# Softplus for the forget gates, a spread start of the first head, four staging buffers for weights, and new places for casts and a scaling

## The chip, the cores and the metric

The kernel runs on one core of a Trainium2 chip. The core has five engines with queues of their own: TensorE (PE, matmuls; PEld is its loading of weights), VectorE (DVE), ScalarE (ACT), GpSimd (POOL) and SyncE (SP), which here issues all DMA transfers. Each engine works off its queue in the order in which the program was laid out, and waits on semaphores for the others. The metric is the device time of one execution in microseconds; given is the median of three executions.

## The reference

Two pre-norm residual layers on a sequence of 1024 rows of width 1024, in float32, and a final RMS norm. The first layer is a gated linear recurrence (RG-LRU, width 1536), the second attention with forget gates (FoX, 16 heads of 64).

```python
def lru_mixer(h, w_in, conv_w, conv_b, wa, ba, wx, bx, a_param, w_out):
    u = h @ w_in
    xb, gate = u[..., :LRU_WIDTH], u[..., LRU_WIDTH:]
    xc = causal_depthwise_conv(xb, conv_w, conv_b)
    r = jax.nn.sigmoid(block_diag_linear(xc, wa, ba))
    i = jax.nn.sigmoid(block_diag_linear(xc, wx, bx))
    log_a = -LRU_C * r * jax.nn.softplus(-a_param)
    a = jnp.exp(log_a)
    mult = jnp.sqrt(-jnp.expm1(2.0 * log_a))
    # hs: h_t = a_t * h_(t-1) + mult_t * i_t * xc_t
    y = hs * jax.nn.silu(gate)
    return y @ w_out

def fox_mixer(h, w_in, b_f, w_out):
    u = h @ w_in                                  # q, k, v, gate, f_logit
    cum = jnp.cumsum(jax.nn.log_sigmoid(f_logit + b_f), axis=1)
    # for each head and block of 128 queries:
    logits = q @ k.T / 8 + (cum_q[:, None] - cum_k[None, :])
    p = jax.nn.softmax(jnp.where(kpos <= qpos, logits, -1e30))
    y = (p @ v) * jax.nn.silu(gate)
    return y @ w_out
```

## The kernel before

**Arithmetic.** Each float32 operand of a large product is split into a high part (a cast, `to_hi`, line 88 on ACT, 94 or 96 on DVE) and a low part, the remainder (`to_lo`, line 99, on DVE or POOL). A product then is three matmuls: high by high, high by low, low by high. All go through `matmul` (line 57) and `transpose` (line 61), so that these lines stand for every matmul of the kernel, and the tile names tell them apart: `ups` and `gps` are inner projections, `gate` the block-diagonal gates of the recurrence, `ops` output projections, `S` the scores, `pt` transposed probabilities, `O` the products of probabilities and values.

**Weights.** `split_weights` (line 101) loads a weight tile into a staging tile `wf`, casts it to `wh` and takes the remainder `wl`. The staging tiles rotate through three buffers under one tag; the same tag is used for the gate weights `wgf` of the recurrence (line 287), the output weights of the first layer (line 352) and the late output weights of the second (line 951). A load that finds no free buffer waits on SP, with all later transfers of SP's queue behind it.

**Attention.** `forget(half)` (line 622) transposes the gate logits of 512 positions into PSUM, forms the logarithm of the sigmoid as min(z, 0) − ln(1 + exp(−|z|)) with three activations and two DVE steps, accumulates it with a scan into `cum`, splits it (`cp`) and writes it to DRAM (`cumd`), from where `load` and `load_q` fetch it as rows 64 and 65 of the operands `T` and `U` of the scores. For each head `maxima(hd, c)` (line 684) makes scores `S` for four blocks of 128 queries, masks them and takes the row maximum in one DVE instruction (line 707), and takes the exponential `p` on ACT (line 712). p(384) below means the block whose p has 384 columns. `weigh(hd, c)` transposes p through PE, splits it into `ph` and `pl`, and multiplies with the values. `scale(hd)` multiplies, on POOL, the gate `sg` by the reciprocal row sums `recb`; `gated` multiplies the head pair's output `yo` by it, on POOL too. Results of the first six head pairs are written to DRAM (`y1d`) and fetched again by `load_y`; those of the last two are split at once by `split_y` into `yhh` and `yhl`.

**Order.** A scheduler places the instructions of all engines by its own simulated timeline; so the place of an instruction in an engine's queue follows from costs and free buffers, not from the order of the code alone. The pool's buffers are part of that. `tc.issue_after(x)` keeps what is in its block behind x; `pe[0]` is the last matmul, `seen[0]` the last exponential of `maxima`. Around this the code weaves generators by hand: `run(order, ...)` takes one character per step, a digit for a step of that generator, a dot for a step of `fill`, which is projection work of later heads (`kq_units`, `g_units`) or, at heads 12 to 15, the output projection (`partial`), and then drains the digit generators. `beside(steps, first, more)` takes a step of `more` with each step from number `first` on. `split_loaded(c)` splits the fetched y tiles, two pairs a step. `values` loads and multiplies the values of four heads; it runs at the end of heads 3, 7 and 11.

## Time and profile before

| | us |
|---|---|
| median of three executions | 1123.55 |
| lowest, highest | 1122.89, 1124.05 |
| profiled execution | 1125.28 |
| its span in the profile | 1123.4 |
| outside the span | 1.88 |

The mean granted clock of TensorE in the profiled execution is 0.997. In the rows of the profile an engine's busy time is given with the number of instructions behind an x; a row of the timeline has its start and length in us, engine, line, operation, output and input with sizes, and in square brackets how long the engine stood idle just before and what ended that.

### The profile page before, as it was taken

To read this page: it belongs to the slowest core of one execution; us is meant where nothing else is said; L and a number is where in the kernel's file an instruction comes from. 1 tells how busy PE (TensorE), PEld (TensorE's weight loads), DVE (VectorE), ACT (ScalarE), POOL (GpSimd) and SP (SyncE) were. 2 spreads that over 40 slices of the span, in tenths; PEclk is the share of its full clock that TensorE was granted. 3 is DMA by queue.
4 is the path that set the end of the run, shared out by engine and by line. 5 is a ranking of instruction groups with operands and counts; after the bars stand their busy time and mean duration, and the time that the engine had idled before them with its cause. 6 is when DMAs were issued, how large, how long until landed. Compare 5 with 4: busy or idle time off the path is not lost. (4 is left out here: it accounts for less than half of the span.)

```text
span 1123.4 us, 15748 instructions
## 1 busy us (share of the span) xinstructions
PE 1106.5 (98%) x5681; PEld 933.0 (83%) x5681; DVE 764.6 (68%) x1271; ACT 589.3 (52%) x1077; POOL 166.5 (15%) x105
## 2 busy tenths in 40 slices
PE   8999999999999999999999999999999999999997
PEld 6787888888888887978888988889888898878886
DVE  7889756776568789666676466764566745676645
ACT  8387445355453666455555355553555534554435
POOL 1311212221121201320010100102001010010110
PEclk9999999999999999999999999999999999999999
DMA  6111111111111114443425214252142431655454
GB/s 218 52 43 51 43 62 38 52 52 44 60 38 52 57 57 144 127 123 100 105 76 133 71 57 119 73 127 81 40 127 79 124 87 38 182 175 162 146 155 187
DMA packets 63702, 105.43 MB, mean 94 GB/s; under 512 B 9508, under 2 KB 24484, under 8 KB 63624
## 3 DMA queue, kind: packets, MB, share of 16 engines
q1 hardware_dynamic: 63624, 104.42, 31.0%
q8 instruction: 45, 0.74, 0.3%
q14 instruction: 33, 0.27, 0.1%
HBM read 63.30 MB, written 15.93 MB: 71 GB/s over the span
## 5 line engine op out<-in xcount | busy, mean ns | idle before, releaser
L57 PE MATMUL gps<-hh,wh 128*128 128x512 f32 x576 | 227.9, 396 | 1.4 <-DVE qkl L585 1.4
L57 PE MATMUL gps<-hl,wh 128*128 128x512 f32 x576 | 225.6, 392 | 0.0
L57 PE MATMUL gps<-hh,wl 128*128 128x512 f32 x576 | 225.5, 391 | 0.0
L88 ACT CAST wh<-wf 128x512 fp32r<-128x512 f32 (+2 forms) x156 | 94.5, 607 | 157.8 <-PE gps L57 48.8
L712 ACT ACTIVATE p<-S,m 128x128 f32<-128x128 f32 (+7 forms) x128 | 95.0, 742 | 124.5 <-DVE m L707 123.6
L99 POOL TENSOR_TENSOR wl<-wf,wh 128x512 fp32r<-128x512 f32 (+1 forms) x60 | 98.1, 1641 | 388.5 <-ACT wh L88 337.4
L99 DVE TENSOR_TENSOR pl<-pt,ph 128x512 fp32r<-128x512 f32 (+1 forms) x198 | 98.7, 540 | 74.4 <-ACT ph L88 73.9
L57 PEld LDWEIGHTS gps<-hl,wh 128*128 128x128 f32 x576 | 108.1, 188 | 23.5
L57 PEld LDWEIGHTS gps<-hh,wh 128*128 128x128 f32 x576 | 108.4, 188 | 20.4 <-DVE qkl L585 1.6
L57 PEld LDWEIGHTS gps<-hh,wl 128*128 128x128 f32 x576 | 108.5, 188 | 19.3 <-POOL wl L99 0.6
L707 DVE CUSTOM_DVE_ANT_0 S<-S,mask 128x128 f32<-128x128 f32 (+7 forms) x128 | 97.2, 760 | 30.5 <-PE S L57 26.0
L739 POOL TENSOR_TENSOR sg<-sg,recb 64x1024 f32<-64x1024 f32 (+1 forms) x17 | 38.9, 2288 | 451.1 <-DMA recb<-recd 415.0
L88 ACT CAST ph<-pt 128x512 fp32r<-128x512 f32 (+1 forms) x198 | 83.5, 472 | 29.7 <-PE pt L61 24.4
L57 PE MATMUL S<-T,U 96*128 96x512 f32 (+7 forms) x384 | 91.9, 348 | 1.8 <-ACT p L712 1.7
L99 DVE TENSOR_TENSOR wl<-wf,wh 128x512 fp32r<-128x512 f32 x96 | 70.4, 735 | 32.0 <-ACT wh L88 31.1
L369 DVE TENSOR_TENSOR x<-x,ops 128x512 f32<-128x512 f32 x80 | 54.1, 682 | 45.6 <-PE ops L57 45.6
L57 PEld LDWEIGHTS S<-T,U 128*128 128x128 f32 (+1 forms) x384 | 68.1, 189 | 15.8 <-ACT p L712 4.2
L61 PE MATMUL pt<-ident,p 128*128 128x128 f32 x576 | 79.5, 273 | 0.4 <-ACT p L712 0.4
L57 PE MATMUL ups<-hh,wh 128*128 128x512 f32 x192 | 75.8, 396 | 2.4 <-ACT hh L90 2.0
L61 PEld LDWEIGHTS pt<-ident,p 128*128 128x128 f32 x576 | 67.1, 140 | 13.3 <-issue 2.2
L57 PE MATMUL ops<-yh,wh 128*128 128x512 f32 x192 | 75.4, 393 | 1.2 <-ACT yh L88 0.6
L57 PE MATMUL ups<-hl,wh 128*128 128x512 f32 x192 | 76.1, 396 | 0.3 <-DVE hl L242 0.2
(177 smaller groups left out, 2258.1 us busy)
## 6 DMA issues: line engine op xcount, KB each, us to landing
wf<-in_w SPq DMA_DIRECT2D x100, 256.0 KB
wf<-in_wo SPq DMA_DIRECT2D x64, 128.0 KB
U<-qkh SPq DMA_DIRECT2D x64, 128.0 KB
T<-qkh SPq DMA_DIRECT2D x28, 256.0 KB
x<-in_xt SPq DMA_DIRECT2D x16, 256.0 KB
x1d<-x SPq DMA_DIRECT2D x16, 256.0 KB
wf<-in_wv SPq DMA_DIRECT2D x16, 256.0 KB
U<-qkl SPq DMA_DIRECT2D x32, 128.0 KB
```

The source lines that it names most:

```text
L57: pe[0] = nc.tensor.matmul(*args, **kw)
L61: pe[0] = nc.tensor.transpose(*args)
L88: nc.scalar.copy(hi, src)
L99: return eng.tensor_tensor(lo, src, f32(hi), ALU.subtract)
L369: nc.vector.tensor_tensor(x, x, pt, ALU.add)
L707: nc.vector.tensor_tensor_reduce(S[:, :n], S[:, :n], mask[:, SEQ - n :], -1.0, -NEG, ALU.add, ALU.min, accum_out=m)
L712: seen[0] = nc.scalar.activation(p, S[:, :n], AF.Exp, bias=m, scale=-1.0, accum_out=sums[:, i : i + 1])
L739: nc.gpsimd.tensor_tensor(sg, sg, recs[hd // 2][rows, cs], ALU.mult)
```

## The change

There are six parts:

- The staging tiles `wf` and `wgf` rotate through four buffers in place of three, at the four places named.
- `forget` negates the bias once on DVE and takes ln(1 + exp(−z)) as one Softplus straight out of PSUM; the scan subtracts it.
- The first head's `maxima(0, 0)` is made before the first fill begins and its steps are spread over two fills; `ordered` is `run` without the draining at the end.
- `scale` works in parts of 512 columns.
- `split_loaded` yields after each pair; the steps at which it begins are 0 and 2 in place of 2 and 4.
- The two calls of `split_y` at heads 13 and 14 stand behind the last exponential.

```diff
--- before.py
+++ after.py
@@ -101,7 +101,7 @@
     def split_weights(src, shape, hi_eng, lo_eng, parts=wpool):
         n = shape[0] * shape[1]
         room = -(-n // 64) * 64
-        a = wpool.tile([P, room], F32, tag="wf", name="wf", bufs=3)[:, :n]
+        a = wpool.tile([P, room], F32, tag="wf", name="wf", bufs=4)[:, :n]
         b = parts.tile([P, room], F32R, tag="wh", name="wh")[:, :n]
         c = parts.tile([P, room], F32R, tag="wl", name="wl")[:, :n]
         wt, hi, lo = (t.rearrange("p (a b) -> p a b", a=shape[0]) for t in (a, b, c))
@@ -284,7 +284,7 @@
             xh, xl = long("xch", F32R), long("xcl", F32R)
             to_hi(xh, xc, nc.scalar)
             to_lo(xl, xc, xh, nc.vector)
-            wt = wpool.tile([P, 4, P], F32, tag="wf", name="wgf", bufs=3)[:, :2]
+            wt = wpool.tile([P, 4, P], F32, tag="wf", name="wgf", bufs=4)[:, :2]
             nc.sync.dma_start(wt, wg[n])
             wgh = tmp.tile([P, 2, P], F32R, tag="wgh", name="wgh")
             wgl = tmp.tile([P, 2, P], F32R, tag="wgl", name="wgl")
@@ -349,7 +349,7 @@
 
         def out_weights(g, d0):
 
-            wt = wpool.tile([P, 4, P], F32, tag="wf", name="wf", bufs=3)
+            wt = wpool.tile([P, 4, P], F32, tag="wf", name="wf", bufs=4)
             for j in range(2):
                 nc.sync.dma_start(wt[:, 2 * j : 2 * j + 2], wo0[d0 + j, :, 2 * g : 2 * g + 2])
             hi = wpool.tile([P, 4, P], F32R, tag="wh", name="wh")
@@ -615,6 +615,7 @@
         Vs = {}
         bft = const.tile([HEADS, 1], F32, name="bft")
         nc.sync.dma_start(bft, bf)
+        nc.vector.tensor_scalar(bft, bft, -1.0, None, ALU.mult)
         unit = at.tile([HEADS, HALF], F32, tag="recb", name="unit", bufs=1)
         nc.gpsimd.memset(unit, 1.0)
         cum = at.tile([HEADS, SEQ], F32, tag="sg", name="cum")
@@ -627,16 +628,12 @@
                     yield
                 with tc.issue_after(pe[0].ins):
                     transpose(pt[:HEADS, i * P : (i + 1) * P], fz[:, half * 4 + i], ident)
-            z_, e_ = (at.tile([HEADS, HALF], F32, tag=t, name=n, bufs=3) for t, n in (("ph", "z"), ("pl", "e")))
+            e_ = at.tile([HEADS, HALF], F32, tag="ph", name="e", bufs=3)
             parts = [at.tile([HEADS, HALF], F32R, tag=f"p{i + 2 * half}", name="cp", bufs=1) for i in (3, 4)]
             hi, lo = parts
-            nc.scalar.activation(z_, pt[:HEADS], AF.Identity, bias=bft)
-            nc.vector.scalar_tensor_tensor(e_, z_, -1.0, z_, ALU.mult, ALU.min)
-            nc.scalar.activation(e_, e_, AF.Exp)
-            nc.scalar.activation(e_, e_, AF.Ln, bias=1.0)
-            nc.vector.scalar_tensor_tensor(z_, z_, 0.0, e_, ALU.min, ALU.subtract)
+            nc.scalar.activation(e_, pt[:HEADS], AF.Softplus, bias=bft, scale=-1.0)
             nc.vector.tensor_tensor_scan(
-                cum[:, cs], unit, z_, cum[:, HALF - 1 : HALF] if half else 0.0, ALU.mult, ALU.add
+                cum[:, cs], unit, e_, cum[:, HALF - 1 : HALF] if half else 0.0, ALU.mult, ALU.subtract
             )
             to_hi(hi, cum[:, cs], nc.vector)
             to_lo(lo, cum[:, cs], hi, nc.vector)
@@ -735,8 +732,10 @@
 
         def scale(hd, cs=slice(0, SEQ)):
             rows = slice((hd % 2) * HD, (hd % 2 + 1) * HD)
-            sg = sgs[hd // 2][rows, cs]
-            nc.gpsimd.tensor_tensor(sg, sg, recs[hd // 2][rows, cs], ALU.mult)
+            for b in range(cs.start, cs.stop, HALF):
+                part = slice(b, b + HALF)
+                sg = sgs[hd // 2][rows, part]
+                nc.gpsimd.tensor_tensor(sg, sg, recs[hd // 2][rows, part], ALU.mult)
 
         def weigh(hd, c, sub=slice(0, HALF)):
 
@@ -809,13 +808,17 @@
 
         seen = [None]
 
-        def run(order, *gens, fill=iter(()), side=iter(())):
+        def ordered(order, *gens, fill=iter(()), side=iter(())):
 
             for i in order:
                 with tc.issue_after(pe[0].ins):
                     next(fill if i == "." else gens[int(i)], None)
                 if i == ".":
                     next(side, None)
+
+        def run(order, *gens, **kw):
+
+            ordered(order, *gens, **kw)
             for g in gens:
                 drain(g)
 
@@ -838,8 +841,7 @@
                 yh, yl = y1[c][pair]
                 to_hi(yh, f32(yl), nc.scalar)
                 to_lo(yl, f32(yl), yh, nc.vector)
-                if pair % 2:
-                    yield
+                yield
 
         def beside(steps, first, more):
 
@@ -948,7 +950,7 @@
             for half in range(2):
                 wh, wl = (kqpool.tile([P, 8, P], F32R, tag=f"qk{p}{half}", name=f"wo{p}") for p in "hl")
                 for b in range(2):
-                    wt = wpool.tile([P, 4, P], F32, tag="wf", name="wf", bufs=3)
+                    wt = wpool.tile([P, 4, P], F32, tag="wf", name="wf", bufs=4)
                     for d in range(2):
                         nc.sync.dma_start(wt[:, 2 * d : 2 * d + 2], wo1[half * 4 + b * 2 + d, :, 6:8])
                     sl = slice(4 * b, 4 * b + 4)
@@ -964,13 +966,14 @@
             next(gates1)
             take(fill, 2)
         drain(gates1)
+        early = maxima(0, 0)
+        ordered(".0.", early, fill=fill)
         drain(fill)
         fill = g_units(0)
-        for _ in range(4):
-            next(fill)
+        ordered("0.", early, fill=fill)
         load(0, halves[1], (1,))
         load(1, halves[1], (1,))
-        run("00.0.0", maxima(0, 0), fill=fill)
+        run("0..0", early, fill=fill)
         load_q(1, 0)
         drain(fill)
         for hd in range(HEADS):
@@ -987,9 +990,9 @@
                         g_units(7, (0,)),
                         load_y(0),
                         first_out(),
-                        beside(g_units(7, (1,)), 2, splits[0]),
+                        beside(g_units(7, (1,)), 0, splits[0]),
                         load_y(1),
-                        beside(beside(partial(todo), 0, splits[0]), 4, splits[1]),
+                        beside(beside(partial(todo), 0, splits[0]), 2, splits[1]),
                         turned(0, 0),
                         turned(0, 1),
                     )
@@ -1000,7 +1003,8 @@
             if hd == HEADS - 1:
                 break
             if hd == 14:
-                split_y(1, 6, yos[6, 1])
+                with tc.issue_after(seen[0].ins):
+                    split_y(1, 6, yos[6, 1])
             scale(hd)
             gated(hd, 0)
             side = late() if hd == 14 else iter(())
@@ -1012,7 +1016,8 @@
             drain(side)
             gated(hd, 1)
             if hd == 13:
-                split_y(0, 6, yos[6, 0])
+                with tc.issue_after(seen[0].ins):
+                    split_y(0, 6, yos[6, 0])
             if hd < 12:
                 drain(fill)
             if hd % 4 == 3 and hd < 12:
```

In the rows below the places of instructions are shown as the two programs have them, in an engine's own order. A number behind a name tells two tiles of that name apart, and is not the same in the two programs.

DVE at the second half of the forget gates and the first head's scores, before (`cum` is the scan's result, `cp` its two parts, `gps` a key or query projection with its parts `qkh` and `qkl`):

```order
L637 SCALAR_TENSOR_TENSOR z<-z,e 16x512
L638 SCALAR_TENSOR_TENSOR cum<-unit,cum,z 16x512
L579 TENSOR_TENSOR gps_4074<-gps_4074,rs_3257 128x512
L94 CAST cp<-cum 16x512
L99 TENSOR_TENSOR wl<-wf,wh 128x512
L96 TENSOR_SCALAR qkh<-gps_4074 128x512
L99 TENSOR_TENSOR cp<-cum,cp 16x512
L585 SCALAR_TENSOR_TENSOR qkl<-gps_4074,qkh 128x512
```

and now, three rows behind the second half's scan, with a remainder `qkl` and the 128x128 maximum between (ISA is the masked maximum, the second ISA row its read-out):

```order
L94 CAST cp<-cum 16x512
L99 TENSOR_TENSOR cp<-cum,cp 16x512
L99 TENSOR_TENSOR wl<-wf,wh 128x512
L579 TENSOR_TENSOR gps_4065<-gps_4065,rs_3257 128x512
L704 ISA S,m<-S,mask 128x256
L704 ISA m 128x1
L99 TENSOR_TENSOR wl<-wf,wh 128x512
L96 TENSOR_SCALAR qkh<-gps_4065 128x512
L704 ISA S,m<-S,mask 128x384
L704 ISA m 128x1
L585 SCALAR_TENSOR_TENSOR qkl<-gps_4065,qkh 128x512
```

The scan has left this stretch for an earlier place, both casts of `cum` stand ahead of the projection, and the maxima of 256 and 384 columns have come in between it and its `qkl`.

ACT at head 3, where the values of heads 4 to 7 are loaded, before (`wh` is a weight's cast, of the values where it stands ahead of the exponentials of 384 and 512 columns):

```order
L88 CAST wh<-wf 128x512
L712 ACTIVATE p,sums<-S,m 128x256
L88 CAST qkh<-gps_4948 128x512
L88 CAST ph<-pt 128x512 x2
L88 CAST wh<-wf 128x512
L712 ACTIVATE p,sums<-S,m 128x384
L88 CAST ph<-pt 128x512
L88 CAST ph<-pt 128x384
L88 CAST wh<-wf 128x512
L712 ACTIVATE p,sums<-S,m 128x512
```

and now:

```order
L88 CAST ph<-pt 128x512
L88 CAST wh<-wf 128x512 x2
L709 ACTIVATE p,sums<-S,m 128x256
L88 CAST ph<-pt 128x512 x2
L88 CAST qkh<-gps_4941 128x512
L88 CAST wh<-wf 128x512
L709 ACTIVATE p,sums<-S,m 128x384
L88 CAST ph<-pt 128x512
L88 CAST ph<-pt 128x384
L88 CAST ph<-pt 128x256
L709 ACTIVATE p,sums<-S,m 128x512
```

The casts of the values' weights have moved up by one block: the first (in the pair) ahead of the exponential of 256 columns, the second ahead of that of 384; none is left ahead of 512. Heads 7 and 11 read alike.

ACT at the end of head 13, with the cast of head pair 6 (`yhh<-yo`), before:

```order
L88 CAST wh<-wf 128x512
L88 CAST wh<-wf 128x256
L88 CAST yhh<-yo 128x512
L712 ACTIVATE p,sums<-S,m 128x384
L88 CAST ph<-pt 128x512
L88 CAST ph<-pt 128x384
L88 CAST wh<-wf 128x512
L712 ACTIVATE p,sums<-S,m 128x512
```

and now:

```order
L88 CAST wh<-wf 128x512
L88 CAST wh<-wf 128x256
L709 ACTIVATE p,sums<-S,m 128x384
L88 CAST ph<-pt 128x512
L88 CAST ph<-pt 128x384
L88 CAST wh<-wf 128x512
L709 ACTIVATE p,sums<-S,m 128x512
L88 CAST yhh<-yo 128x512
```

The cast of `yo`, which waits for POOL, has gone from the place ahead of the exponential of 384 columns to the place behind that of 512.

## The prediction

> **What bounds the kernel now.** I read the busy times first, then TensorE's (PE's) waits, then the same busy times cut into stages, and only then single rows.
>
> ```profile
> PE 1106.5 (98%) x5681; PEld 933.0 (83%) x5681; DVE 764.6 (68%) x1271; ACT 589.3 (52%) x1077; POOL 166.5 (15%) x105
> ```
>
> PE is busy for 1106.5 of 1123.4 us. The change neither adds nor removes a matmul, so all it can give is part of the 16.9 us in which PE stands, or a second effect of such a stand on the clock.
>
> ```profile
> PE S L57 <- ACT p L712: 1.7, 2, 1.2
> PE gps L57 <- DVE qkl L585: 1.4, 1, 1.4
> PE gate L57 <- DVE wgl L99: 1.4, 1, 1.4
> 98.00:103.00 5.00, 3.07 (x11) 1.84 (x12) 5.00 (x6) 4.95 (x7) 1.55 (x2) 1.00 0.09 26
> 440.00:520.00 80.00, 78.56 (x446) 67.99 (x445) 54.31 (x101) 41.69 (x78) 22.93 (x18) 1.00 0.42 118
> 520.00:600.00 80.00, 79.64 (x425) 66.63 (x424) 54.23 (x116) 43.18 (x99) 10.41 (x5) 1.00 0.36 100
> 600.00:975.00 375.00, 374.51 (x2186) 326.91 (x2185) 228.53 (x485) 185.73 (x424) 40.02 (x20) 1.00 0.33 89
> 975.00:1060.00 85.00, 82.90 (x424) 69.04 (x422) 59.06 (x116) 42.72 (x94) 7.70 (x4) 1.00 0.59 184
> 1060.00:1123.40 63.40, 57.64 (x318) 48.27 (x316) 34.35 (x74) 28.08 (x74) 5.34 (x5) 0.97 0.47 161
> ```
>
> A wait row gives the total, the times and the longest; a stage row its length, then the busy time of PE, PEld, DVE, ACT and POOL, the granted clock, DMA share and GB/s. Idle time of PE lies at a few places: 1.93 us at 98–103, 1.44 at 440–520, 0.36 at 520–600, 0.49 at 600–975, 2.10 at 975–1060. The last stage, 5.76, contains the final stores, and no order around it changes much. So the change is worth what it does at four places: A the recurrent layer near 100 us, B the forget gates near 500, C the loads of the next heads' values near 593, 735 and 877, D the last heads near 990–1048.
>
> **The change part by part.**
>
> *B, softplus and the spread maxima.*
>
> ```profile
> 492.38 1.28 ACT L635 ACT_TABLE_LOAD   x1
> 496.73 0.63 ACT L636 ACTIVATE e<-e 16x512 f32<-16x512 f32 x1
> 497.39 0.68 DVE L637 SCALAR_TENSOR_TENSOR z<-z,e 16x512 f32<-16x512 f32 x1 [1.25 <-ACT e L636]
> 498.11 1.27 DVE L638 TENSOR_TENSOR_SCAN cum<-unit,cum,z 16x512 f32<-16x512 f32 x1
> 499.31 0.66 DVE L579 TENSOR_TENSOR gps<-gps,rs 128x512 f32<-128x512 f32 x1
> 502.02 0.67 DVE L585 SCALAR_TENSOR_TENSOR qkl<-gps,qkh 128x512 fp32r<-128x512 f32 x1
> 502.75 0.50 PE L57 MATMUL gps<-hh,wh 128*128 128x512 f32 x1 [1.44 <-DVE qkl L585]
> ```
>
> PE at 502.75 waits for a PSUM buffer that qkl frees. qkl came late because DVE, in order, stood 1.25 us for the Ln, then ran z, the scan, both casts of cum and one weight remainder with the gps product among them. In the new order the chain Identity, table, Exp, table, Ln with two DVE steps is one activation, so the scan runs some 5 us earlier (from before the table load at 492.38 to the scan at 498.11 is 5.7 us; Softplus takes an estimated 0.65 of them, the row nearest to it being the 0.63 of the Exp or Ln form). The casts of cum then stand ahead of the gps product. What moves in front of qkl instead are maxima, 0.28 to 0.56 us each, when their S is there. Replaying DVE's new queue with these durations, qkl ends near 499, and PE asks for its buffer near 501.4. The stall goes whole: 1.44 us, and 0.11 because the first matmul took 0.50 instead of 0.39: **−1.55**. If it goes only in part, three maxima before qkl (1.3 us) could put back up to that: ends −1.55 and −0.3. What is late next is the first S, which now comes some 11 us sooner and needs this half's T and U; those wait for cumd of the first half, whose chain also gets shorter, so I count no new wait. ACT saves three table loads of 1.28 us, two Exp/Ln pairs and more; this lies beside PE, as ACT is busy for only 52%. The new negation of a 16x1 tile is a tiny DVE step long before its use: nothing.
>
> *C, a fourth staging buffer.* It lets a weight load be issued one tile earlier, and the scheduler then places the casts of the loaded tiles one step earlier too.
>
> ```profile
> 583.31 0.36 SPq L109 DMA_DIRECT2D wf<-in_wv  x1
> 588.02 0.36 SPq L109 DMA_DIRECT2D wf<-in_wv  x1
> 592.20 0.62 ACT L88 CAST wh<-wf 128x512 fp32r<-128x512 f32 x1 [3.01 <-DMA wf<-in_wv]
> 592.73 0.57 ACT L712 ACTIVATE p<-S,m 128x384 f32<-128x384 f32 x1
> 592.85 0.69 DVE L99 TENSOR_TENSOR wl<-wf,wh 128x512 fp32r<-128x512 f32 x1 [1.82 <-ACT wh L88]
> 593.57 0.33 SPq L109 DMA_DIRECT2D wf<-in_wv  x1
> 596.57 0.62 ACT L88 CAST wh<-wf 128x512 fp32r<-128x512 f32 x1 [2.32 <-DMA wf<-in_wv]
> 598.80 0.38 PE L57 MATMUL O<-pl,v 128*128 128x256 f32 x1 [0.24 <-DVE pl L99]
> ```
>
> A value load takes 3.0 us (593.57 to 596.57) to 4.2 (588.02 to 592.20) until its cast. Two of these casts stand in ACT's queue ahead of p(384) and p(512). PE's idle time in this stage is 0.36 in all, 0.24 of it at 598.80; slower first matmuls behind the stops bring the price of the place to an estimated 0.6. In the new order the first cast stands right behind the casts of p(128) and the second ahead of p(384), with its remainder wl (0.69) ahead of that block's maximum on DVE; and its load can be issued only when the first tile's remainder has been taken. The first load is issued at 583.31 and there by about 586.9 (3.6 us, between the two rows); with a cast of 0.6 and a remainder of 0.7 the second load goes out near 588.3. If that takes 3.0 us, what follows (to the remainder 0.65, to the maximum 0.6, to p 0.7, p itself 0.57) ends near 593.9, against 593.30 now (592.73 and 0.57). PE is then about 0.6 later than now at p(384), a wait of some 0.9, and loses nothing at 598.80: net +0.2 to +0.3 a site, **+0.7** for the three, which I take: SP's new order has another weight load, which waits for a buffer of its own, ahead of T's loads, so this one starts out alone and is nearer to the row of 3.0. If the load takes 4.2, p comes 1.2 later still: +1.4 a site, +4.3 in all. If the load is early enough, all three lose their stops: −1.5.
>
> *D, y's casts and POOL's scaling.*
>
> ```profile
> 990.34 0.55 PE L61 MATMUL pt<-ident,p 128*128 128x128 f32 x3 [0.41 <-ACT p L712]
> 1002.90 2.39 POOL L739 TENSOR_TENSOR sg<-sg,recb 64x1024 f32<-64x1024 f32 x1 [40.01 <-DMA recb<-recd]
> 1003.04 2.80 DVE L99 TENSOR_TENSOR wl<-wf,wh 128x512 fp32r<-128x512 f32 x1 [0.50 <-ACT wh L88]
> 1007.03 0.62 ACT L88 CAST yhh<-yo 128x512 fp32r<-128x512 f32 x1 [2.88 <-POOL yo L794]
> 1007.55 0.57 ACT L712 ACTIVATE p<-S,m 128x384 f32<-128x384 f32 x1
> 1008.27 0.73 PE L57 MATMUL S<-T,U 128*128 128x512 f32 x2 [1.16 <-ACT p L712]
> 1045.12 0.41 ACT L88 CAST wh<-wf 128x256 fp32r<-128x256 f32 x1 [1.95 <-DMA wf<-in_wo]
> 1045.56 1.23 DVE L99 TENSOR_TENSOR wl<-wf,wh 128x256 fp32r<-128x256 f32 x1 [0.47 <-ACT wh L88]
> 1046.72 0.56 DVE L707 CUSTOM_DVE_ANT_0 S<-S,mask 128x384 f32<-128x384 f32 x1
> 1048.09 0.74 PE L57 MATMUL S<-T,U 128*128 128x512 f32 x2 [0.53 <-ACT p L712]
> ```
>
> At 1007.03 ACT stands 2.88 us with the cast of yo, which waits for POOL, and p(384) behind it. The cast now follows p(512), so p(384) waits for its own maximum alone. That maximum is late too, by the remainder of 2.80 us at 1003.04 that ran beside POOL's scaling of 2.39. Split in two parts, the scaling should let DVE in between, and p is in time: −1.16 and −0.1 of slower first matmuls. If the remainder stays that long, p(384) starts near 1007.0 instead of 1007.55: −0.5. I take **−1.15**, since the remainder's length went with that scaling. POOL does the same elements in two instructions, and is busy for 15%: nothing.
>
> By the Trainium skill (SBUF — State Buffer, SBUF: two separate sides), DVE with two SBUF inputs and GpSimd take a shared port as an exclusive lock for a whole instruction. By that rule a remainder waits for half a scaling, an estimated 1.2 us, and the place at 1008 is worth −1.15; were the port shared by rate, it would be −0.5. The rows fit the lock: the remainder ends 0.55 us after POOL.
>
> At 1048.09 the wait is one chain: a late load, cast 1045.12, remainder 1.23 (beside a scaling again), maximum 1046.72, p. That cast and the one before it now both stand ahead of p(256) and the remainder leaves the place ahead of the maximum: **−0.6** (0.53 and a slower step; ends −0.7, and +0.5 if ACT then waits for the load with p(256) behind it). At 990.34 the loaded y tiles are now split pair by pair and one more remainder, about 0.7 us, stands ahead of the 896 maximum, of which something is hidden: **+0.3** (ends −0.4 and +0.7).
>
> *A, the order near 100 us.*
>
> ```profile
> 99.90 1.48 DVE L99 TENSOR_TENSOR wgl<-wgf,wgh 128x256 fp32r<-128x256 f32 x1
> 101.31 1.21 DVE L99 TENSOR_TENSOR yl<-a,yh 128x1024 fp32r<-128x1024 f32 x1
> 101.44 0.73 PE L57 MATMUL gate<-xch,wgl 128*128 128x512 f32 x2 [1.41 <-DVE wgl L99]
> 99.46:102.88 3.42, 1.84 (x7) 1.00 0.10 27
> 102.88:106.29 3.41, 3.41 (x10) 0.52 0.43 122
> ```
>
> The fourth buffer also reorders this stage: yl goes ahead of wgl on DVE, and PE runs the yl products before the gate products. Both still have to be made, DVE has no gap here, and a weight remainder is put further ahead: PE still waits for the later of the two. Bounds −1.0 and +1.0; I take **0**. The last two rows (PE alone, granted clock behind it) show a second cost: after a stretch with PE busy for 1.84 of 3.42 us the clock was half for the next one, in which 10 matmuls ran instead of 16, about 1.4 us lost.
>
> The sum is 0 − 1.55 + 0.7 − 1.15 − 0.6 + 0.3 = **−2.3 us**. The profiled execution took 1125.28, 1.73 above the median of 1123.55; the terms are the same in each, so that execution would become 1122.98, and the median 1121.25, which I give as **1121.2**.
>
> **The rivals.**
>
> *Slower: value loads late at all three C places.* ACT then stands in order with p behind it, three times, and this decides the sign from the point where a load takes about 4 us to its cast, with the other gains in part. Against: the row of 3.0 us, and a slot that comes free sooner with four. For: the row of 4.2. With C at +4.3, A at +1, B and the 1008 place in part (−0.6, −0.5) and D's others 0, the sum is +4.2: 1127.7.
>
> *The half clock goes too.* If PE's idle at 99–103 is cut or falls across two of the 3.41 us stretches, 1.4 us more are gained, and the sum is −3.7: 1119.9. Against: nothing there removes work. For: the 1.44 us at 502.75 was idle as well and drew no half clock, so a stand of that size alone does not suffice.
>
> The Trainium skill (TensorE: Matmul & The Clock Gate, Part 1) says the gate judges free-running windows of 3413 ns. The trace agrees in length, 3.41. By that rule a shift of under a microsecond can move the stand over a window's edge, and the half clock with it; the result would be the 1119.9 just worked out.
>
> *The waits move and the gain is not there.* B's stall turns into one on the first S or its T and U, or p at 1008 stays behind another cast: −1.55 becomes −0.3, or −1.15 becomes 0, and the whole about −0.8: 1122.7.
>
> **How the numbers follow.** Forecast 45% (1121.2; it spans 1120.2 to 1122.2 by its smaller terms), half clock gone 20% (1119.9), waits only moved 27% (1122.7), slower 8% (1127.7). About 0.2% of the time, 2.25 us, is what a measurement of this kernel can tell from no change, so the bounds are 1121.3 and 1125.8. Faster: 0.27 of the forecast's 0.45 and 0.20: 0.47. Same: 0.18, 0.27: 0.45. Slower: 0.08. The range takes the first three cases with the ends of their unknown costs: 1118.6 (half clock gone, and C at −0.6) to 1124.2 (waits moved, and C 1.5 worse).
>
> **What would show it.** B: no wait row PE gps from qkl, one table load for Softplus and one for the next Exp. D: the S waits for p at 1008 and 1048 gone, and remainders beside POOL's scaling near 1.2 instead of 2.80. C: ACT's idle on wf<-in_wv ahead of p(384) and a longer S wait there. A: a row of half clock, or none. I am wrong if B's 1.44 us shows up under another name within 20 us, or if C's S waits pass 2 us each.

## The result and the profile after

| | before | changed |
|---|---|---|
| median of 6 executions, us | 1123.44 | 1118.83 |
| lowest, highest | 1121.80, 1124.86 | 1116.88, 1119.86 |
| profiled execution, its span | 1125.28, 1123.4 | 1119.86, 1118.1 |

The ratio is 0.9956, with a 95% interval of 0.9946 to 0.9966: 4.6 us faster by the medians and 4.9 by the ratio, where 2.35 were forecast. A second set of the same two kernels gave 1118.88 against 1124.93, ratio 0.9948 (0.9932 to 0.9965).

The busy times of the changed kernel; then a stretch of the opening, with the columns PE, granted clock, DMA share and GB/s; then TensorE's waits and the stages, with the same columns as before:

```profile
PE 1104.4 (99%) x5681; PEld 934.2 (84%) x5681; DVE 758.0 (68%) x1268; ACT 583.4 (52%) x1070; POOL 170.1 (15%) x120
10.20:13.60 3.40, 3.33 (x8) 0.54 1.07 403
PE S L57 <- ACT p L709: 1.6, 2, 0.9
PE ops L57 <- DVE yl L99: 1.6, 1, 1.6
PE pt L61 <- ACT p L709: 0.8, 1, 0.8
98.00:103.00 5.00, 3.36 (x15) 2.50 (x14) 5.00 (x6) 4.95 (x7) 1.76 (x2) 1.00 0.00 0
103.00:107.00 4.00, 4.00 (x19) 3.27 (x19) 4.00 (x4) 0.84 (x1) 1.81 (x1) 1.00 0.64 196
440.00:520.00 80.00, 80.00 (x460) 70.05 (x459) 50.98 (x103) 36.77 (x75) 22.30 (x18) 1.00 0.40 115
520.00:600.00 80.00, 80.00 (x428) 67.24 (x427) 55.23 (x115) 44.07 (x100) 11.53 (x8) 1.00 0.39 105
600.00:975.00 375.00, 373.31 (x2179) 325.65 (x2178) 230.88 (x485) 185.54 (x423) 42.57 (x30) 1.00 0.33 91
```

No row is left of PE waiting for qkl or for wgl, and the stages 440–520 and 520–600 are full. Near 100 us one wait on yl stands in place of three, and the clock behind it is 1.00 where it was 0.57: 19 matmuls run in 103–107 in place of 12. The stage 600–975 has lost 1.2 us more than before, at the value loads of heads 7 and 11. And the opening has a stretch of half clock, with 8 matmuls, that the profile of before does not have.

Both traces hold 5681 matmuls, so the n-th of the one can be set against the n-th of the other. Their difference in start, taken ahead of and behind each place, gives what the place is worth; the columns are the forecast, this profile and a second profile of the changed kernel (run e2_change_again), each against the one profile of before, in us:

| place | forecast | first | second |
|---|---|---|---|
| opening, to 50 us | 0 | +1.6 | 0.0 |
| A, 93 to 109 | 0 | −2.8 | −2.9 |
| B, 464 to 507 | −1.55 | −1.8 | −2.1 |
| C, 575 to 985, with the three value loads | +0.7 | +0.1 | −0.3 |
| D at 990 | +0.3 | +0.4 | +0.6 |
| D at 1008 | −1.15 | −1.5 | −1.5 |
| D at 1048 | −0.6 | −0.8 | −0.8 |

With some tenths between the places these make the whole, −5.3 and −7.3.

### The profile page after: what moved, and what is told of

The parts are those of the page before. It is cut to its first block, busy times and chain, and to the rows that moved or that the text cites. A ratio compares the mean times of both kernels' runs of the same rounds, so it can differ in the third digit from the quotient of the medians.

```text
span 1118.1 us, 15738 instructions
## 1 busy us (share of the span) xinstructions
PE 1104.4 (99%) x5681; PEld 934.2 (84%) x5681; DVE 758.0 (68%) x1268; ACT 583.4 (52%) x1070; POOL 170.1 (15%) x120
## 4 chain that ended last, share of the span: by engine, by line
PE 89%; DVE 6%; DMA 2%; ACT 2%; issue 1%; POOL 0%; SPq 0%; DVEq 0%; ACTq 0%
PE gps L57 32%; PE ops L57 16%; PE ups L57 9%; PE vps L57 8%; PE S L57 6%; PE O L57 6%; PE pt L61 5%; PE turn L57 3%; PE gate L57 2%; DMA wf<-in_wv 1%; DVE xc L283 1%; DMA x<-in_xt 0%; ACT wh L88 0%; DVE wl L99 0%; DVE a L336 0%
## 5 line engine op out<-in xcount | busy, mean ns | idle before, releaser
L738 POOL TENSOR_TENSOR sg<-sg,recb 64x512 f32<-64x512 f32 x32 | 43.4, 1375 | 448.1 <-DMA recb<-recd 448.1
L57 PE MATMUL ops<-yl,wh 128*128 128x512 f32 x192 | 73.9, 390 | 1.6 <-DVE yl L99 1.6
```

Of the source, the lines that this page charges most:

```text
L57: pe[0] = nc.tensor.matmul(*args, **kw)
L738: nc.gpsimd.tensor_tensor(sg, sg, recs[hd // 2][rows, part], ALU.mult)
```

## The experiments

Each kernel was timed beside the kernel before, in four sets; all ratios are to the times of before in the same set. Where matmul starts are compared, it is one profile of the run against the one profile of before.

| run | median, us | ratio (95%) |
|---|---|---|
| e1_buffers | 1122.68 | 0.9986 (0.9975 to 0.9996) |
| e1_all_but_buffers | 1120.10 | 0.9958 (0.9942 to 0.9973) |
| e1_forget | 1122.83 | 0.9985 (0.9971 to 0.9999) |
| e1_tail | 1120.98 | 0.9969 (0.9959 to 0.9979) |
| e2_change_again | 1118.88 | 0.9948 (0.9932 to 0.9965) |
| e2_fill_the_stand | 1122.34 | 0.9981 (0.9971 to 0.9991) |
| e2_y_casts_alone | 1121.60 | 0.9971 (0.9960 to 0.9983) |
| e2_values_held | 1119.10 | 0.9951 (0.9934 to 0.9967) |
| e3_softplus_alone | 1123.43 | 0.9994 (0.9981 to 1.0007) |
| e3_late_y_split | 1118.73 | 0.9950 (0.9934 to 0.9966) |
| e3_best | 1115.49 | 0.9919 (0.9904 to 0.9933) |
| e4_values_late_only | 1116.08 | 0.9934 (0.9917 to 0.9950) |

### The parts by themselves

The fourth buffer alone (four places, on the kernel before):

```diff
-        a = wpool.tile([P, room], F32, tag="wf", name="wf", bufs=3)[:, :n]
+        a = wpool.tile([P, room], F32, tag="wf", name="wf", bufs=4)[:, :n]
...
-            wt = wpool.tile([P, 4, P], F32, tag="wf", name="wgf", bufs=3)[:, :2]
+            wt = wpool.tile([P, 4, P], F32, tag="wf", name="wgf", bufs=4)[:, :2]
```

> Only the fourth staging buffer, all else as before. Theory (the ledger of the two traces: the buffer carries what happened at the opening, near 100 us and at the value loads): the wait on the yl products near 100 us is one of about 1.8 us with no half clock behind it, so PE gains about 2.8 us there; the opening costs 0.4 us, or 1.6 with a half clock at 10 to 14 us; the value loads near 593, 735 and 877 us come out about even; together 1.0 to 2.5 us faster than before (ratio 0.9978 to 0.9991). Rival (the gain near 100 us came from another part, or from the chance of the clock's windows): stage near 100 us as before, wait on wgl of 1.4 us, and the time the same or up to 1 us slower.

The stage near 100 us came as the theory says: the matmuls behind it start 2.8 us earlier. So it is the buffer that makes that order. Some of TensorE's waits in this kernel:

```profile
PE S L57 <- ACT p L712: 3.1, 4, 1.8
PE pt L61 <- DVE pl L99: 1.9, 2, 1.2
PE ops L57 <- DVE yl L99: 1.6, 1, 1.6
PE gps L57 <- DVE qkl L585: 0.2, 1, 0.2
```

The first two rows lie at the value loads of heads 3, 7 and 11 and at 1006 us. At head 3 a remainder of the weights stood beside POOL's scaling:

```profile
582.90 2.69 POOL L739 TENSOR_TENSOR sg<-sg,recb 64x1024 f32<-64x1024 f32 x1 [14.91 <-DMA recb<-recd]
583.84 2.29 DVE L99 TENSOR_TENSOR wl<-wf,wh 128x512 fp32r<-128x512 f32 x1
```

It took 2.29 us at head 11 too, and 0.68 at head 7, where it was first. By the starts head 3 costs 0.6 us, head 11 1.4, the place at 990 0.6 and that at 1008 0.7; head 7 gains 0.5 and 1048 0.8. The opening cost nothing here (−0.6). The row of gps is the wait that B is about: it is down from 1.4 to 0.2 us without Softplus, and the stretch from 464 to 507 us is 1.2 us shorter. By the medians the kernel is 1.9 us faster, in the range expected, and so by less than the one stage gained.

The change with the old three buffers (the diff above taken the other way on the changed kernel):

> The whole change with three staging buffers. Theory: the stage near 100 us is as before, with 1.4 us of wait on wgl and a stretch of half clock; the opening is as before; the wait on qkl near 502 us (1.44) is gone, as are the waits for p near 1008 and 1048; 3 to 4 us faster than before (ratio 0.9964 to 0.9973). Rival (the fourth buffer is what makes room for the new order near 500 and 1008): less than 2 us faster.

The stage near 100 us is as before, with its half clock; the waits on qkl and at 1008 us are gone; the one at 1048 stays (0.75 us by the starts). It is 4.5 us faster, more than the 3 to 4 expected, and with 0.9958 as fast as the whole change within what is measured. By the starts the buffer adds to the other parts a gain of 0.8 us at 1048 and 1.3 near 100 us, the half clock left out, and a loss of 0.5 to 0.7 at the value loads and 990. That about 1.5 us is left of it in the times is not shown.

Softplus and spread maxima alone (the hunks on `forget`, `ordered` and `early`):

> Only the Softplus and the spread maxima of the first head. Theory: the wait on qkl near 502 us is gone and nothing else moves: 1.5 to 2.1 us faster (ratio 0.9981 to 0.9987). Rival (the gain there needs the fourth buffer's earlier weight loads): some of the 1.44 us returns under another name, under 1 us faster.

The theory holds at its place: there is no wait on qkl, and the stretch from 464 to 507 us is 2.0 us shorter. But the rest did move: near 100 us no half clock followed (−1.75 by the starts), and at 1008 a wait of 1.85 us and a stretch of half clock cost 2.2 us.

The last heads' parts alone (`scale`, `split_loaded`, `beside` and both `split_y`):

> Only the parts of the last heads: the scaling in two parts, the pair-by-pair split of loaded y tiles, the later casts of y. Theory: the waits for p near 1008 and 1048 us are gone (1.4 and 0.7 us by matmul starts), the one near 990 is 0.4 us longer: 1.5 to 1.9 us faster (ratio 0.9983 to 0.9987). Rival (the 1048 gain comes from the fourth buffer, which loads the late output weights sooner): the wait near 1048 stays at 0.5 us or more and the gain is 1.0.

The waits at 990 and 1008 are gone, the one at 1048 stays (1.05 us). So the rival was right on 1048: that gain is the buffer's. The total is better than the 1.5 to 1.9 us expected, with a mean clock of 0.9986 in its 12 executions against 0.9974 in the 29 of before; what that means is the next question.

### The half clock

Three of these kernels (before, e1_tail and e1_all_but_buffers) have the same order near 100 us and the same waits. Their clocks differ. First the kernel with the last heads' parts, then the one with three buffers (columns as in the opening's row):

```profile
99.50:103.00 3.50, 1.82 (x7) 1.00 0.19 53
103.00:107.00 4.00, 4.00 (x19) 1.00 0.34 117
```

```profile
99.50:102.00 2.50, 1.03 (x4) 0.98 0.05 12
102.00:106.00 4.00, 4.00 (x11) 0.58 0.44 142
```

PE stands for about 1.5 to 1.7 us in both, and only in the second does a half clock follow: 11 matmuls in 4 us in place of 19. The time of it is 1.4 to 1.5 us.

The Trainium skill (TensorE: Matmul & The Clock Gate, Part 1) says that the gate judges free-running windows of about 3.4 us. The trace agrees in length: in the profile of before the clock went to full at 4.05 us, to half at 103.03 and back at 106.44, 29 times and once 3.41 us later. With the windows laid out from such changes, PE was busy for 1.83 (before), 1.76 (e1_all_but_buffers) and 1.71 us (e2_y_casts_alone) of the window ahead of a half clock. It was busy for 1.90 (e1_tail) and 1.96 us (e3_softplus_alone) where none followed, and in e1_forget the stand fell on two windows, 2.64 and 2.62 us busy, and none followed. These six have PE's old order. With the fourth buffer's order the stand lay in one window too, as in the profile of the change:

```profile
99.25:102.66 3.41, 1.77 (x8) 1.00 0.00 0
102.66:106.08 3.42, 3.42 (x17) 1.00 0.59 169
```

Six profiles with that order have such a window, 1.77 to 1.84 us busy, and in none did a half clock follow. So the busy time of the window does not decide it alone. Either the new order brings it more rarely, or it was chance six times; that stays open.

> The changed kernel once more, unaltered, for a second profile and more times. Theory (a stretch of half clock, 1.4 us, falls where a stand of PE happens to lie in one of the clock's free windows): the stands near 5 to 10 us and at 102 us are there again, and the half clock at 10 to 14 us is not, or not in the same place; executions with a lower mean clock are longer, about 1.1 us for each 0.001. Rival (the fourth buffer's early weight load causes it): half clock at 10 to 14 us again and in nearly every execution a mean clock of 0.998 or less. In both the wait on the yl products near 102 us is 1.6 to 1.8 us and the median 1118 to 1120.

The half clock at 10 to 14 us was not there again, and the mean clock of the six executions was 0.9992 on average: the rival falls. But lower clocks did not go with longer times in these six: the one with 0.998 took 1117.9 us, the two with 1.000 took 1117.3 and 1119.7.

In the kernel before they do. Of its 29 executions beside the first four experiments, with mean clocks from 0.994 to 1.000, the five with 0.999 took 1123.3 us on average and the seven with 0.997 took 1125.1: 0.9 us for each 0.001; a straight line through all 29 gives 0.7. One stretch of half clock takes 0.0015 off the mean (half of 3.41 in 1120 us).

The other test is to take the stand away and leave the order. Six products are made that nobody needs:

```diff
                     pt = ps.tile([P, HALF], F32, tag="O", name="gate")
+                    for _ in range(3 if n == 3 and j == 0 else 0):
+                        matmul(pt, w[0], s["x"][0][:, cs], start=True, stop=True)
                     gemm(pt, [(w, tuple(z[:, cs] for z in s["x"]))])
```

> The kernel before with six more matmuls, products of the gate that are computed again and overwritten, between the gate's two high products and the wait on wgl near 100 us; nothing is left out. Theory (idle time of PE in one window brings the half clock): PE is busy while it would wait, the products with wgl start within 0.3 us of the time they had, and no half clock follows near 103 us; that saves up to 1.4 us in the executions that had it, about 0.7 us of the median up to 107 us. Rival (the half clock there has another cause): it still follows in the profile. The order behind 110 us differs from before in places, so the total is not compared closely.

PE's timeline, and then its windows:

```profile
98.77 2.01 PE L57 MATMUL gate<-xch,wgh 128*128 128x512 f32 x8
100.95 0.73 PE L57 MATMUL gate<-xch,wgl 128*128 128x512 f32 x2 [0.18 <-DVE wgl L99]
```

```profile
99.40:102.80 3.40, 3.05 (x13) 1.00 0.22 57
102.80:106.20 3.40, 3.40 (x17) 1.00 0.39 122
```

The wait of 1.41 us is 0.18, wgl is ready when it was, and no half clock follows. Of 12 executions 10 have a mean clock of 0.999, where of the 23 of before beside them 6 have 0.999 or more, and the median is 2.6 us under that of before, with more work in it. By the profile the part up to 109 us gives 1.4 of it; the order further on differs too and is not told apart.

### The wait for p(384) at 1008 us

The late casts of y alone, with the scaling in one piece:

```diff
             if hd == 14:
-                split_y(1, 6, yos[6, 1])
+                with tc.issue_after(seen[0].ins):
+                    split_y(1, 6, yos[6, 1])
...
             if hd == 13:
-                split_y(0, 6, yos[6, 0])
+                with tc.issue_after(seen[0].ins):
+                    split_y(0, 6, yos[6, 0])
```

> Only the two late casts of y; the scaling stays in one piece. Theory (the cast that waits for POOL ahead of p(384) is the whole cause): the wait of S for p near 1006 us is gone though the scaling is whole, whichever of POOL and DVE starts first unless POOL is first by a hair: 1.2 to 2.0 us faster than before. Rival (the prediction's: the remainder beside the undivided scaling keeps p late): at least 0.5 us of wait stays, under 0.9 us faster.

Rows of POOL, DVE, ACT and PE there:

```profile
1003.05 2.38 POOL L739 TENSOR_TENSOR sg<-sg,recb 64x1024 f32<-64x1024 f32 x1 [40.49 <-DMA recb<-recd]
1002.17 0.69 DVE L99 TENSOR_TENSOR wl<-wf,wh 128x512 fp32r<-128x512 f32 x1 [0.52 <-ACT wh L88]
1003.49 0.56 DVE L707 CUSTOM_DVE_ANT_0 S<-S,mask 128x384 f32<-128x384 f32 x1
1004.13 0.58 ACT L712 ACTIVATE p<-S,m 128x384 f32<-128x384 f32 x1 [0.85 <-DVE m L707]
1006.08 0.63 PE L57 MATMUL S<-T,U 128*128 128x512 f32 x2
```

The scaling is whole, 2.38 us, and the wait is gone. The remainder started 0.9 us ahead of it and took 0.69. In the profile of before the scaling was ahead by 0.14, and the remainder took 2.80. Of six profiles with the scaling in one piece only one more is like that: in e2_fill_the_stand the scaling was ahead by 0.03, and the remainder took 2.91. In the other four the remainder was first and took 0.69. So this run does not show what a late cast of y is worth where POOL is first. By the starts the place gave 1.4 us. The median is 3.3 us under that of before, more than expected; the mean clock of its ten executions, 0.9986 against 0.9973 in the 23 of before, may account for a part.

The next run leaves that cast in its old place. It is Softplus alone, with the first head's maxima together as before (the negation of the bias is cut here):

```diff
-            nc.scalar.activation(z_, pt[:HEADS], AF.Identity, bias=bft)
...
+            nc.scalar.activation(e_, pt[:HEADS], AF.Softplus, bias=bft, scale=-1.0)
             nc.vector.tensor_tensor_scan(
-                cum[:, cs], unit, z_, cum[:, HALF - 1 : HALF] if half else 0.0, ALU.mult, ALU.add
+                cum[:, cs], unit, e_, cum[:, HALF - 1 : HALF] if half else 0.0, ALU.mult, ALU.subtract
```

> Only the Softplus with the subtracting scan; the first head's maxima stay together. Theory (the long chain of the logarithm is what kept qkl late; the spreading adds nothing): the wait on qkl near 502 us is gone as with both parts, and the stretch from 464 to 507 us is about 2 us shorter than in the profile of before. Rival (the spreading carries part of it, or the maxima packed behind the gates bring a wait of their own): 0.3 us or more of wait left near 500 to 505 us.

The theory holds at its place: no wait near 502 us, 1.8 us gained from 464 to 507. So the spreading isn't needed for it. But the time is that of before: in the profiled execution the old place at 1008 takes 3.4 us, more than all of it, back. POOL, ACT and PE there:

```profile
1000.98 2.38 POOL L736 TENSOR_TENSOR sg<-sg,recb 64x1024 f32<-64x1024 f32 x1 [41.93 <-DMA recb<-recd]
1003.44 1.26 POOL L791 TENSOR_TENSOR yo<-yo,sg 128x512 f32<-128x512 f32 x1
1004.74 0.62 ACT L88 CAST yhh<-yo 128x512 fp32r<-128x512 f32 x1 [4.74 <-POOL yo L791]
1005.98 0.73 PE L57 MATMUL S<-T,U 128*128 128x512 f32 x2 [3.02 <-ACT p L709]
```

Here one reads the chain of that wait: the reciprocals' DMA, the scaling, the product, the cast, and behind the cast p(384), ready for 4 us. PE stood 3.02 us, with a stretch of half clock behind it. With the cast in its old place the wait was 1.16 (before), 1.27 (e2_fill_the_stand), 1.81 (e1_buffers), 1.85 (e1_forget) and 3.02 us in five profiles: it is the end of a DMA and two POOL steps against PE, and varies with them. The profile of before, from which the forecast was made, had the shortest.

### The value loads and the y tiles

In the changed kernel the second value load's cast stands ahead of p(384), as forecast. ACT and PE at head 7:

```profile
729.60 0.62 ACT L88 CAST wh<-wf 128x512 fp32r<-128x512 f32 x1 [1.30 <-DMA wf<-in_wv]
731.51 0.58 ACT L709 ACTIVATE p<-S,m 128x384 f32<-128x384 f32 x1 [1.29 <-DVE m L704]
732.23 0.50 PE L57 MATMUL S<-T,U 128*128 128x512 f32 x1 [0.78 <-ACT p L709]
```

At head 3 such a cast runs at 587 us, and the values' own products begin at 617.7. So the casts were held, here behind p(1024):

```diff
-        to_hi(b, a, hi_eng)
+        if hold:
+            with tc.issue_after(hold[-1].ins):
+                to_hi(b, a, hi_eng)
+        else:
+            to_hi(b, a, hi_eng)
...
+                if not ex and k > 2:
+                    hold.append(seen[0])
                 parts += split_weights(
...
+                hold.clear()
```

> The change with the last two casts of the values' weights held behind p(1024) at heads 3, 7 and 11; the fourth buffer stays. Theory (these casts, which wait for a load ahead of p(256) and p(384), are all that the fourth buffer costs there): the waits near 590, 732 and 875 us, 0.2, 0.95 and 1.0 us in the profile of the change, are gone, and with them 1 to 2 us: ratio to before 0.994 to 0.995. Rival (the casts turn up late for the values' own products or push something else): a wait of PE near 618 us or another near 605, no gain over the change.

The waits are gone and the rival's came, at three places; ACT and PE at the first:

```profile
604.45 1.13 ACT L88 CAST wh<-wf 128x512 fp32r<-128x512 f32 x2
605.48 0.54 ACT L88 CAST ph<-pt 128x256 fp32r<-128x256 f32 x2
606.96 0.39 PE L57 MATMUL O<-pl,v 128*128 128x256 f32 x1 [0.67 <-DVE pl L99]
```

Two casts, 1.13 us, now stand ahead of ph, which PE needs at once, and with 0.9951 the time is that of the change. The y tiles were held in the same way:

```diff
-                to_hi(yh, f32(yl), nc.scalar)
+                if c:
+                    with tc.issue_after(seen[0].ins):
+                        to_hi(yh, f32(yl), nc.scalar)
+                else:
+                    to_hi(yh, f32(yl), nc.scalar)
```

> The change with the casts of the six loaded y tiles of the second half held behind the newest exponential, so that fewer remainders of y stand ahead of the maximum of 896 columns. Theory (these remainders make the wait for p(896) near 986 us, 1.0 and 1.2 us in the two profiles of the change): that wait is gone, no other appears, about 1 us faster than the change. Rival (another step holds that maximum, or the casts come late for the output projection): the wait stays, or PE waits for yhh near 992 to 998 us.

The wait for p(896) is gone and 0.7 us on pl has come at 988.72 in its place; no gain. Then both, with the values' casts moved once more:

```diff
-                if k == (2 if ex else KT - 2):
+                if k == 2 or (k > 2 and not ex):
                     yield
...
                 next(vals)
+
+                def held_values(vals=vals):
+                    for i in range(0 + 2):
+                        if i >= 0:
+                            hold.append(seen[0])
+                            next(vals)
+                            hold.clear()
+                        yield
+
+                side = held_values()
             run(second, weigh(hd, 1), maxima(hd + 1, 0), fill=fill, side=side)
```

At its first step `seen[0]` is p(128) of the next head.

> The change, with the casts of the y tiles held as in the run before, and the last two casts of the values' weights held behind p(128) of the next head rather than p(1024) of this one (heads 3, 7, 11). Theory: with p(1024) the two casts stood ahead of the casts ph of the last blocks, which gave the new wait of 0.94 us near 607, 749 and 891; behind p(128) nothing urgent follows, so all of these waits and those at 732 and 873 us are gone, 2.5 to 3 us faster than the change (ratio to before 0.992 to 0.994). Rival (wherever the two casts stand, some p or ph behind them is urgent): waits of 0.5 us or more near 610 to 620 us and no gain from this part.

Its waits, the longest first, and none of them at the value loads:

```profile
PE ops L57 <- DVE yl L99: 1.6, 1, 1.6
PE warm L57 <- DVE epst L70: 1.1, 1, 1.1
PE ups L57 <- ACT hh L90: 0.7, 1, 0.7
PE O L57 <- DVE pl L99: 0.7, 1, 0.7
```

With 1115.49 it beats both kernels: the change by 3.3 us by the medians of two sets, and 0.9919 stands against 0.9956 and 0.9948. The last run takes the y tiles' holding out again:

> The change with the values' last two casts held behind p(128) of the next head, and the y tiles split as in the change. Theory (the whole gain of the best version is the value casts'; holding the y tiles only moved a wait of 0.9 us from p(896) to pl): no wait of PE for p near 590, 732 and 873 us, the wait for p(896) near 984 us of 1.0 to 1.3 us is back, and the median is within 0.6 us of the best version's 1115.5. Rival (holding the y tiles gave part of it): 1116.3 to 1117.

The median is 1116.08, and the wait for p(896) is back with 1.1 us. The gain is the values' casts': by the starts the stretch from 575 to 985 us is 1.6 us shorter than before, where the change has +0.1 and −0.3. That holding y adds nothing is within what is measured, not shown; the ratios, 0.9934 and 0.9919, leave room for a gain.

## Why the prediction was off

**The bound** was read rightly: all that was gained was time in which PE stood, and what follows from it.

**A is the step that failed.** It was put at nothing and measured −2.8 and −2.9, more than the 2.4 us between the forecast of 1121.2 and the result. "Both still have to be made, DVE has no gap here ... PE still waits for the later of the two. Bounds −1.0 and +1.0; I take 0." PE's waits there, in the profile of before the first and the third of three (the second is the 1.41 for wgl), and then in that of the change the only one:

```profile
98.35 0.50 PE L57 MATMUL ops<-yh,wh 128*128 128x512 f32 x1 [0.65 <-ACT yh L88]
...
102.58 0.85 PE L57 MATMUL ops<-yl,wh 128*128 128x512 f32 x2 [0.17 <-DVE yl L99]
```

```profile
102.25 0.73 PE L57 MATMUL ops<-yl,wh 128*128 128x512 f32 x2 [1.64 <-DVE yl L99]
```

The later of the two it is, 1.64 us for yl. But the text left out the first wait, 0.65 for yh, ahead of which PE's new order has other matmuls, and three starts after a stop in place of one. The order is worth −1.3, which is −2.8 less the 1.5 of the clock. e1_buffers shows that the buffer makes it; e1_tail, with the old order and no half clock, gains 1.5 there and no more.

**The half clock** was a rival with 20%, "if PE's idle at 99–103 is cut or falls across two" windows. Only the first was so, by a little: PE's idle time at 98–103 went from 1.93 to 1.64 us, and all of it lay in one window, 1.77 us busy where before had 1.83. So that its sum, 1119.9, is nearer to the result than the forecast is in part luck. The fault was to treat the half clock as one event that stays or goes. In the old order it comes in some executions and not in others, and the profile of before had drawn it, which the forecast then kept as fixed: e1_tail and e1_all_but_buffers have the same stand without and with it, and e2_fill_the_stand has neither stand nor half clock. The mean clock was 0.9974 over 29 executions of before and 0.9983 and 0.9992 in the two sets of the change; at 0.7 to 0.9 us for 0.001 that would be 0.6 to 1.6 us of the gain. This is an estimate and not shown: the medians of the two sets of the change, 1118.83 and 1118.88, do not differ as their clocks do.

**B** held in its mechanism: all five profiles without Softplus have a wait on qkl, none of the nine with it has, and Softplus alone does it. The table loads are the two that were named, at 474.39 and 491.99 us, and the first S brought no new wait. The size, −1.8 and −2.1 for −1.55, came out near in part by luck: the 1.44 us of before is the longest of the five waits (the others are 0.21 to 0.87), and in e1_buffers, e1_tail and e2_y_casts_alone the stretch is 0.6 to 1.2 us shorter than before without Softplus. Against these three it is worth 0.6 to 1.5 us.

**C** came in part as forecast and was too high in sum: the waits for p(384) at heads 7 and 11 came, 0.95 and 1.03 us by the starts, but at head 3 nothing was waited for and 0.9 us was gained, and the whole stretch made +0.1 and −0.3 in place of +0.7. e4_values_late_only shows that the same load brings no wait for p(384) with its cast elsewhere. The forecast did not have POOL in it. In three profiles (two of the change, and e3_late_y_split) the second remainder of the loaded weights took 1.18 to 1.37 us beside the scaling at heads 7 and 11, where p(384) came late, and 0.68 at head 3, where it did not. With the three heads of e1_buffers, the longer remainder goes with the late p, or there with the lost time, at all twelve places; that it causes it, and that a scaling in parts saves time there, no run shows by itself.

**D at 1008** came out near (−1.5 for −1.15) for a reason that was half wrong. The cast's place alone does it, with the scaling undivided, where DVE's remainder is first. The forecast took the remainder of 2.80 for the rule, and that row came of a close race; for such an execution "−0.5 if the remainder stays that long" was not tested. No run tells apart what the scaling's division does to the time. On a remainder it shows: in e1_tail one of 128x256, alone 0.42 us long, started 0.31 us behind the scaling in parts and took 1.27, near the 1.2 that was forecast, while in e1_buffers, e1_forget and e2_y_casts_alone it started 0.9 to 1.0 behind the whole scaling and took 1.68 to 1.75. The Trainium skill's rule of the exclusive port (SBUF — State Buffer, SBUF: two separate sides) still agrees with the rows: in the changed kernel DVE's remainder was first here, and POOL's two parts took longer than at the next head.

```profile
1000.22 3.15 POOL L738 TENSOR_TENSOR sg<-sg,recb 64x512 f32<-64x512 f32 x2 [40.99 <-DMA recb<-recd]
1040.31 2.53 POOL L738 TENSOR_TENSOR sg<-sg,recb 64x512 f32<-64x512 f32 x2 [25.00 <-DMA recb<-recd]
```

```profile
1000.03 0.69 DVE L99 TENSOR_TENSOR wl<-wf,wh 128x512 fp32r<-128x512 f32 x1 [0.49 <-ACT wh L88]
```

Which of the two starts first decides which of them waits; here that was not on the path.

**D at 990 and 1048** held (+0.4, +0.6 for +0.3; −0.8 for −0.6), but both are the buffer's doing, by e1_buffers, e1_tail and e1_all_but_buffers, and not that of the parts under which the prediction put them.

**The slower rival** (value loads late at three places) did not come together. The lost time of e1_buffers at heads 3 and 11 looks like it, but what is longer there than at head 7 is the remainder beside the scaling, 2.29 us for 0.68.

## What to carry to other kernels

An engine that works in order should not hold an instruction that waits for a load or a slow engine ahead of one that the bound engine needs: the waits at 1008 us and at the value loads were casts of that kind, and both were cured by where the cast stands, not by its cost. But move it until nothing urgent is behind it, or the wait only changes its name (held behind p(128) in place of p(1024) the same casts gave 1.9 us more by the ratios of e4_values_late_only and e2_values_held). And where the granted clock has dropped once in a profile, look at the clocks of all executions before a sum is made against that one.

## What was not expected of the hardware

A stand of PE can cost more than its length: about 1.6 us of idle time in a window of 3.41 us was followed by 3.41 us of half clock in some profiles (before, e1_all_but_buffers), at 1.4 to 1.5 us a time, and 1.5 us was not in e1_tail. In the fourth buffer's order 1.6 us never was, in six profiles. Windows with less than 1.6 us of busy time (1.56 in e1_forget, 1.32 in e3_softplus_alone, both at 1005 us) were followed by it. Six matmuls of no use in that stand, 1.4 us of PE's work, went with a kernel 2.6 us faster, of which 1.4 lie at that place.
